# Modulation of the first layer split between TensorE and VectorE, vectors stored as rows, weight splits on ScalarE and GpSimd

## The chip, the cores and the metric

The kernel runs on one core of a Trainium2 chip. The metric is the device time of one execution in microseconds (us). The core's engines are TensorE (PE, with its weight loads PEld), VectorE (DVE), ScalarE (ACT), GpSimd (POOL) and SyncE (SP), which here issues nearly all DMAs. Each engine works through its own queue in order and waits on semaphores of the others.

## The reference

Two layers over 2048 latent tokens and 256 context tokens of width 1024. Cut to what matters here:

```python
silu_c, silu_cc = silu(c), silu(c_ctx)            # two condition vectors, 1024 long
for l in range(2):
    shift, scale, gate = split(silu_c @ w_mod[l] + b_mod[l], 3)        # w_mod[l]: 1024 x 3072
    shift_c, scale_c, gate_c = split(silu_cc @ w_mod[l] + b_mod[l], 3) # the same for the context
    hx = rmsnorm(x, norm_g[l]) * (1 + scale) + shift
    hy = rmsnorm(y, norm_g[l]) * (1 + scale_c) + shift_c
    # hx, hy @ w_in[l]: columns for a Fourier mix, a gated MLP over chunks, and attention (q, k, v, gate)
    # three branches, each times its SiLU gate, concatenated, then
    x = x + gate * (concat(f, g, o) @ w_out[l])
    # and, in the first layer alone, y = y + gate_c * (...)
```

Everything is in float32. The kernel keeps that accuracy by splitting each operand into a high and a low half of fewer bits (`hi` = rounded copy, `lo` = operand minus `hi`) and multiplying three times (high by high, high by low, low by high).

## The kernel before

The kernel is written as a list of operations in program order; a planner (`Plan`) then simulates the engines with a table of costs and writes each engine's queue in the order in which its simulation started the operations. Where several are ready, the one earlier in program order goes first. An operation also needs its tiles: each tile name has a fixed number of buffers in a pool, and a pool opens and closes at a mark that waits until all of its users are done in the plan. So program order is a priority, and a moved statement moves in all queues. Since all instructions are issued by one line of `Plan.emit`, every row of the profile says L447, and groups are told apart by tile names.

A layer runs in stages. *Modulation*: shift (`sh`), scale (`gs`) and gate (`gc`) are made for both conditions `c2` (columns of 128, eight chunks of the 1024, two conditions). *Projection*: tokens go in blocks of 4, 4, 2, 2 and 6 tiles of 128. `norm` loads a tile, normalises it, transposes it on TensorE, applies scale and shift (half on VectorE, half on ScalarE) and splits it; `block` then runs the tile against five groups of weight columns. `group` loads a group of 8 chunks of 128 rows (416, 512, 256, 512 and 512 columns for groups 0 to 4), and `resident` scales each by a power of two (`wr`) taken from the largest entry (`am`, `power`) and splits it in place. Groups 0 and 1 live in tiles called `h`, the others in `w`; the scaled copy is a `k` tile (tiles `k1`, `k2`, `k3` and `k5` all print as `k`). *Attention* follows, with a background of Fourier mixing, the layer's gate vector (`modulate_turned` on VectorE, then `gates`) and, in layer 0, `prepare` for layer 1. *Output*: `outward` projects, multiplies by the gate row `gr` and adds to x; during it `modulate_turned` makes shift and scale for layer 1.

In layer 0 `modulate` makes shift, then scale: for each half of 512 columns eight loads of 128 x 512 weights and eight matmuls with the two conditions as the stationary operand, then a copy and four small transposes back into columns. It is called for shift, then two tiles are fetched ahead, then for scale. `bounded` derives the common scaling. `c_d` and `g_d` are scratch rows in DRAM: conditions and gates are stored there from their column layout, and read back broadcast to all partitions.

In layer 0 program order is then: `norm` of the first four tiles, group 0, and `prepare` (the small weights).

The lines that order the start:

```python
modulate(0, y, (0,), k2)
ahead = {t: fetch(0, t) for t in range(2)}
modulate(0, y, (1,), k2)
...
sp.dma_start(out=c_d[c].rearrange("(k p) -> p k", k=KC), in_=c2[:, :, c])
...
for t in BLOCKS[0][0]:
    hts[t] = norm(0, y, t, ahead.get(t))
wt = {0: group(0, y, 0, wp)}
```

Of the kernel before, what the change touches and what calls it, by code (L numbers as in the profile page):

```python
# [10 lines left out]
F32 = mybir.dt.float32  # L11
F32R = mybir.dt.float32r
F16 = mybir.dt.float16
BF16 = mybir.dt.bfloat16
I32 = mybir.dt.int32
AF = mybir.ActivationFunctionType
ALU = mybir.AluOpType
# [4 lines left out]
P = 128  # L22
# [526 lines left out]
def hybrid_kernel(ctx: ExitStack, tc: tile.TileContext, a: dict, out: bass.AP):  # L549
# [3 lines left out]
    def mk(p, shape, dt, tag, bufs=None):  # L553
        return plan.tile(p, shape, dt, tag, bufs or p.bufs)

    def opened(name, side, bufs=2):
        p = plan.pool(name, bufs=bufs, side=side, reuse_waits="tile")
        p.bufs = bufs
        return p
# [17 lines left out]
    def bank(shape=None, tag="cb"):  # L577
        return mk(stage[0] if tag in ("pj", "cx", "sc") else ps, shape or [P, NB], F32, tag, BANKS[tag])
# [113 lines left out]
    def column(i):  # L692
        return cols[:, i:i + 1]


    NAMES, BASES = ("sh", "gs", "gc"), (C_BSH, C_BSC, C_BG)

    def modulated(l, y, part, ns, sums):

        co = l * C_L  # L700
        dst = y[NAMES[part]]
        b0 = co + BASES[part] + ns.start
        for c in range(2):
            dve.tensor_tensor(out=dst[:, ns, c], in0=sums[:, :, c], in1=cols[:, b0:b0 + ns.stop - ns.start], op=ALU.add)
            if part == 1:
                dve.scalar_tensor_tensor(out=dst[:, ns, c], in0=dst[:, ns, c], scalar=1.0,
                                         in1=cols[:, co + C_G + ns.start:co + C_G + ns.stop], op0=ALU.add, op1=ALU.mult)

    def modulate(l, y, parts, load):

        for part in parts:
            y[NAMES[part]] = mk(lay, [P, KC, 2], F32, NAMES[part], 1)
            for n in range(2):
                row = bank([2, NB])
                for k in range(KC):
                    wm = load()
                    sp.dma_start(out=wm, in_=a["w_mod"][l, k * P:(k + 1) * P, part * D + n * NB:part * D + (n + 1) * NB])
                    pe.matmul(row, c2[:, k, :], wm, start=k == 0, stop=k == KC - 1)
                o = bank([P, 4, 2])
                rs = load()[0:2, :]  # L720
                act.activation(out=rs, in_=row, func=AF.Copy)
                with plan.group():
                    for m in range(4):
                        pe.transpose(o[:, m], rs[:, m * P:(m + 1) * P], ident[0:2, 0:2])
                modulated(l, y, part, slice(4 * n, 4 * n + 4), o)

    def modulate_turned(l, y, parts, load):

        conds = []
        for c in range(2):  # L730
            for n in range(2):
                w = load()
                sp.dma_start(out=w, in_=c_d[c, n * NB:(n + 1) * NB].partition_broadcast(P))
                conds.append(w)
        for part in parts:
            y[NAMES[part]] = mk(lay, [P, KC, 2], F32, NAMES[part], 2 if part == 2 else 1)
            acc = mk(lay, [P, 2, KC, 2], F32, "acc")
            for k in range(KC):
                for n in range(2):
                    wm = load()  # L740
                    sp.dma_start(out=wm, in_=a["w_modT"][l, part * D + k * P:part * D + (k + 1) * P, n * NB:(n + 1) * NB])
                    for c in range(2):
                        jk = k2([P, D], BF16)[:, :NB]
                        dve.scalar_tensor_tensor(out=jk, in0=wm, scalar=1.0, in1=conds[2 * c + n], op0=ALU.mult, op1=ALU.mult,
                                                 accum_out=acc[:, n, k, c:c + 1])
                    yield
            dve.tensor_tensor(out=acc[:, 0], in0=acc[:, 0], in1=acc[:, 1], op=ALU.add)
            modulated(l, y, part, slice(0, KC), acc[:, 0])
# [45 lines left out]
    def whole(v):  # L794

        return v.rearrange("p s n -> p (s n)").bitcast(F32)
# [103 lines left out]
    def fetch(l, t):  # L900
        xt = k5()[:, :D]
        sp.dma_start(out=xt, in_=src(l, t))
        return xt

    def norm(l, y, t, xt=None):
        c = 1 if t < CT else 0
        xt = xt or fetch(l, t)
        jk = k2([P, D], BF16)
        ss = mk(small, [P, 1], F32, "ss")
        act.activation(out=jk, in_=xt, func=AF.Square, accum_out=ss)  # L910
        dve.tensor_scalar(out=ss, in0=ss, scalar1=1.0 / D, scalar2=EPS, op0=ALU.mult, op1=ALU.add)
        rs = rsqrt1(ss)
        dve.tensor_scalar(out=xt, in0=xt, scalar1=rs, scalar2=-1.0, op0=ALU.mult, op1=ALU.mult)
        hh, hl = rows_operand(t)
        for half in range(2):
            tp = bank([P, 4, P], "cx" if half else "cb")
            with plan.group():
                for i in range(4):
                    k = 4 * half + i
                    pe.transpose(tp[:, i], xt[:, k * P:(k + 1) * P], ident)  # L920
            u = k2([P, 4, P])
            for i in range(4):
                k = 4 * half + i
                if half:
                    act.activation(out=u[:, i], in_=tp[:, i], func=AF.Identity, scale=y["gs"][:, k, c:c + 1], bias=y["sh"][:, k, c:c + 1])
                else:
                    dve.tensor_scalar(out=u[:, i], in0=tp[:, i], scalar1=y["gs"][:, k, c:c + 1], scalar2=y["sh"][:, k, c:c + 1],
                                      op0=ALU.mult, op1=ALU.add)
            s = slice(4 * half, 4 * half + 4)
            act.activation(out=hh[:, s], in_=u, func=AF.Copy)  # L930
            pool.tensor_tensor(out=hl[:, s], in0=u, in1=hh[:, s], op=ALU.subtract)
        return hh, hl
# [16 lines left out]
    def resident(y, g, parts, v):  # L949


        am = mk(small, [P, KC + 1], F32, "am", 2)
        for k in range(KC):
            c0 = 0
            for get, c in parts:
                get(k, whole(v(k))[:, c0:c0 + c])
                c0 += c
            dve.tensor_reduce(out=am[:, k:k + 1], in_=whole(v(k)), axis=AX.X, op=ALU.max, apply_absolute_value=True)
        dve.tensor_tensor(out=am[:, :KC], in0=am[:, :KC], in1=y["hi"], op=ALU.mult)
        dve.tensor_reduce(out=am[:, KC:], in_=am[:, :KC], axis=AX.X, op=ALU.max)  # L960
        pw = mk(lay, [P, 2], F32, f"pw{g}")
        power(am[:, KC:], pw)
        y["ic"][g] = pw[:, 1:]
        r = mk(small, [P, KC], F32, "wr", 2)
        dve.tensor_scalar(out=r, in0=y["hi"], scalar1=pw[:, 0:1], scalar2=None, op0=ALU.mult)
        n = v(0).shape[2]
        for k in range(KC):
            w = k2()[:, :n]
            if k % 2:
                dve.tensor_scalar(out=w, in0=whole(v(k)), scalar1=r[:, k:k + 1], scalar2=None, op0=ALU.mult)  # L970
            else:
                act.activation(out=w, in_=whole(v(k)), func=AF.Copy, scale=r[:, k:k + 1])
            act.activation(out=v(k)[:, 0], in_=w, func=AF.Copy)
            (pool if k % 2 else dve).tensor_tensor(out=v(k)[:, 1], in0=w, in1=v(k)[:, 0], op=ALU.subtract)
        return [(v(k)[:, 0], v(k)[:, 1]) for k in range(KC)]

    def weights(parts, wp, scale=None, extra=None):
# [645 lines left out]
    def gates(l, y, pc):  # L1623

        y["gr"] = []
        for c in range(1 if l == DEPTH - 1 else 2):
            sp.dma_start(out=g_d[c].rearrange("(k p) -> p k", k=KC), in_=y["gc"][:, :, c])
            gr = mk(pc, [P, D], F32, f"gr{c}", 1)
            sp.dma_start(out=gr, in_=g_d[c].partition_broadcast(P))
            y["gr"].append(gr)  # L1630
# [10 lines left out]
        sp.dma_start(out=out[(t - CT) * P:(t - CT + 1) * P, ns] if l == DEPTH - 1 else x1_d[t][:, ns], in_=xr)  # L1641


    def run(jobs):
        for _ in jobs:
            pass

    banks("project")
    wp = opened("W", "right")
    pa = opened("A", "left")  # L1650
    y = {}
    modulate(0, y, (0,), k2)
    ahead = {t: fetch(0, t) for t in range(2)}
    modulate(0, y, (1,), k2)
    tt = mk(cst, [P, 2, 256], F32, "tt")
    sp.dma_start(out=tt, in_=a["dft64"])
    for c in range(2):
        sp.dma_start(out=c_d[c].rearrange("(k p) -> p k", k=KC), in_=c2[:, :, c])
    hts = {}
    bounded(y)  # L1660
    pa_[0] = pa
    for t in BLOCKS[0][0]:
        hts[t] = norm(0, y, t, ahead.get(t))
    y["ic"] = [None] * 5
    wt = {0: group(0, y, 0, wp)}
    first = prepare(0, y, wp)
    for _ in range(8):
        next(first)
# [189 lines left out]
```

## Time and profile before

| | |
|---|---|
| runs (3) | median 3200.58 us, 3195.83 to 3202.14 |
| profiled execution | 3200.15 us, span 3198.0 us |
| mean granted TensorE clock | 0.969 |
| busy: TensorE, weight loads | 2978.9 us (93%), 1737.2 us (54%) |
| busy: VectorE, ScalarE, GpSimd | 2463.7 us (77%), 1811.3 us (57%), 1674.5 us (52%) |
| DMA | 291.69 MB, mean 91 GB/s; 377744 of 495312 packets under 512 B |

Busy shares are means over stages with different limits. The first projections begin at about 80 us, layer 0's attention runs from about 640 to 1460 us, layer 1's first projections are at about 1715 us. A view of windows gives busy time by stage; a row of the timeline gives start, duration, engine and operation; the chain that ended last is followed back from the last instruction.

### The profile page before, as it was taken

To read this page: it belongs to the slowest core of one execution; us is meant where nothing else is said; L and a number is where in the kernel's file an instruction comes from. 1 tells how busy PE (TensorE), PEld (TensorE's weight loads), DVE (VectorE), ACT (ScalarE), POOL (GpSimd) and SP (SyncE) were. 2 spreads that over 40 slices of the span, in tenths; PEclk is the share of its full clock that TensorE was granted. 3 is DMA by queue.
4 is the path that set the end of the run, shared out by engine and by line. 5 is a ranking of instruction groups with operands and counts; after the bars stand their busy time and mean duration, and the time that the engine had idled before them with its cause. 6 is when DMAs were issued, how large, how long until landed. Compare 5 with 4: busy or idle time off the path is not lost.

```text
span 3198.0 us, 64363 instructions
## 1 busy us (share of the span) xinstructions
PE 2978.9 (93%) x23200; PEld 1737.2 (54%) x23200; DVE 2463.7 (77%) x6739; ACT 1811.3 (57%) x3860; POOL 1674.5 (52%) x1816
## 2 busy tenths in 40 slices
PE   5799999899999999998999899998999999999899
PEld 1355555445655455556785454553455555555687
DVE  4888788789998978864638988986898989887332
ACT  2553345267677788884005544531787878888500
POOL 1453444457667777772003645542776777777300
PEclk7899999999999999999999999998999999999999
DMA  8323344532224322205535343445123222230342
GB/s 269 61 59 68 71 86 85 104 106 71 73 76 134 71 64 55 77 22 165 180 116 188 57 91 81 88 94 128 36 62 89 72 83 67 75 80 18 111 128 83
DMA packets 495312, 291.69 MB, mean 91 GB/s; under 512 B 377744, under 2 KB 427024, under 8 KB 494992
## 3 DMA queue, kind: packets, MB, share of 16 engines
q1 hardware_dynamic: 492112, 282.34, 34.3%
q0 software_dynamic: 2880, 5.24, 0.6%
q8 instruction: 182, 2.98, 0.4%
q14 instruction: 138, 1.13, 0.1%
HBM read 195.80 MB, written 91.66 MB: 90 GB/s over the span
## 4 chain that ended last, share of the span: by engine, by line
PE 58%; DVE 20%; DMA 9%; ACT 6%; POOL 3%; SPq 3%; issue 2%; DVEq 0%; ACTq 0%; POOLq 0%
PE pj L447 17%; PE sc L447 17%; PE pv L447 11%; PE mx L447 9%; DVE k L447 6%; DVE mx L447 3%; PE cb L447 3%; SPq L447 3%; DMA k<-d 2%; ACT k L447 2%; DVE ns_t L447 1%; POOL k L447 1%; ACT pp L447 1%; DMA k<-in_x_dram 1%; DMA mw<-in_w_modT_dram 1%
## 5 line engine op out<-in xcount | busy, mean ns | idle before, releaser
L447 POOL TENSOR_TENSOR pp<-pw,pp 128x512 f16<-128x512 f32 (+1 forms) x876 | 1021.3, 1183 | 390.0 <-ACT pw L447 313.6
L447 PEld LDWEIGHTS <-h 128*128 128x128 f16 (+2 forms) x7008 | 577.5, 97 | 778.9 <-issue 412.4
L447 DVE TENSOR_REDUCE mx<-mx 128x1 f32<-128x512 f32 (+1 forms) x1296 | 772.6, 626 | 151.2 <-PE mx L447 144.7
L447 ACT ACTIVATE pp<-sc 128x512 f16<-128x512 f32 (+1 forms) x1168 | 716.5, 614 | 243.2 <-PE sc L447 218.0
L447 PE MATMUL sc<-h,h 128*128 128x512 f16 (+1 forms) x2336 | 602.3, 380 | 3.9 <-ACT pw L447 2.1
L447 ACT ACTIVATE pw<-sc 128x512 f32<-128x512 f32 (+1 forms) x876 | 542.7, 620 | 0.6 <-POOL pp L447 0.6
L447 PEld LDWEIGHTS <-pp 128*128 128x128 f16 x10432 | 468.5, 98 | 115.5 <-issue 27.8
L447 PE MATMUL pv<-k,pp 128*128 128x65 f16 (+2 forms) x10432 | 508.3, 203 | 9.2 <-DVE sm L447 7.6
L447 PE MATMUL mx<-h,h 96*128 96x512 f16 (+1 forms) x1296 | 409.5, 367 | 40.0 <-DVE mx L447 25.3
L447 PE MATMUL pj<-wh,h 128*128 128x512 f32 x1088 | 362.9, 406 | 7.9 <-DVE k L447 7.8
L447 PEld LDWEIGHTS <-hp 128*128 128x128 f16 x1920 | 189.6, 100 | 179.0 <-issue 24.6
L447 PE MATMUL pj<-w,h 128*128 128x512 f16 (+1 forms) x1296 | 271.5, 348 | 5.4 <-DVE tm L447 2.1
L447 PE MATMUL pj<-w,hp 128*128 128x512 f16 (+1 forms) x1152 | 244.4, 348 | 10.7 <-DVE tm L447 3.8
L447 PEld LDWEIGHTS pj<-wh,h 128*128 128x128 f32 x1088 | 208.5, 192 | 58.1 <-DVE k L447 11.8
L447 DVE TENSOR_TENSOR pp<-sc,pp 128x512 f16<-128x512 f32 (+1 forms) x292 | 197.9, 678 | 45.1 <-ACT sc L447 41.2
L447 PE MATMUL sc<-h 40*128 40x512 f16 (+1 forms) x1168 | 227.7, 387 | 0.0
L447 PE MATMUL pj<-wl,h 128*128 128x512 f32 x544 | 216.7, 398 | 0.0
L447 PE MATMUL pj<-h,h 128*128 128x416 f16 (+2 forms) x912 | 197.7, 357 | 9.4 <-DVE h L447 5.2
L447 ACT ACTIVATE k<-pj,pw 128x256 f32<-128x256 f32 (+3 forms) x242 | 105.2, 458 | 178.4 <-PE pj L447 166.6
L447 POOL TENSOR_TENSOR h<-k,h 128x512 f16<-128x512 f32 (+1 forms) x56 | 66.4, 1199 | 263.1 <-ACT h L447 263.0
L447 DVE TENSOR_TENSOR pj<-pj,gr 128x512 f32<-128x512 f32 x68 | 47.3, 697 | 190.3 <-PE pj L447 190.3
L447 PE MATMUL pj<-h,hp 128*128 128x416 f16 (+1 forms) x768 | 176.3, 369 | 8.8 <-ACT k L447 5.4
(260 smaller groups left out, 4013.5 us busy)
## 6 DMA issues: line engine op xcount, KB each, us to landing
d<-k SPq DMA_DIRECT2D x560, 48.0 KB
d<-k SPq DMA_DIRECT2D x166, 128.0 KB
d<-k SPq DMA_DIRECT2D x70, 256.0 KB
k<-d SPq DMA_DIRECT2D x132, 128.0 KB
k<-d SPq DMA_DIRECT2D x66, 256.0 KB
h<-d SPq DMA_DIRECT2D x24, 432.0 KB
d<-vt SPq DMA_DIRECT2D x144, 65.0 KB
k<-d SPq DMA_DIRECT2D x16, 585.0 KB
```

The lines of the kernel that those rows point to most:

```text
L447: r = getattr(getattr(self.nc, eng), method)(*args, **kw)
```

## The change

The first layer's shift is no longer a row of matmuls: both conditions are spread to all partitions (identity scaled by each chunk, times a matrix of ones, into four PSUM banks), and VectorE multiplies rows of the transposed weights (`w_modT`) with them and sums along the row. Scale stays on TensorE. One load brings 128 x 1024 weights instead of 128 x 512, from a pool of its own (`pm`, ten buffers) that closes ahead of the pool `wp` for weights. The broadcast conditions also give the rows for `c_d`, and gates are transposed on TensorE so that `g_d` is written in pieces of 128 numbers. `resident` scales all chunks on ScalarE and subtracts all on GpSimd. Group 0 stands ahead of the norms in program order, and no tile is fetched ahead.

```diff
-    def modulate(l, y, parts, load):
-        for part in parts:
+    def modulate(y, load):
+        conds = [bank(tag=tag) for tag in ("mx", "mx", "pj", "pj")]
+        for i in range(2 * KC):
+            dg = k1()[:, :P]
+            dve.tensor_scalar(out=dg, in0=ident, scalar1=c2[:, i % KC, i // KC:i // KC + 1], scalar2=None, op0=ALU.mult)
+            pe.matmul(conds[i // 4][:, i % 4 * P:(i % 4 + 1) * P], ones, dg, start=True, stop=True)
+        for i, o in enumerate(conds):
+            r = k2()[0:1]
+            act.activation(out=r, in_=o[0:1], func=AF.Copy)
+            sp.dma_start(out=c_d[i // 2, i % 2 * NB:(i % 2 + 1) * NB].unsqueeze(0), in_=r)
...
+        halves = [bank([2, NB], "cx" if n else "pv") for n in range(2)]
+        for k in range(KC):
+            wm = load()
+            sp.dma_start(out=wm, in_=a["w_mod"][0, k * P:(k + 1) * P, D:2 * D])
             for n in range(2):
...
+                pe.matmul(halves[n], c2[:, k, :], wm[:, n * NB:(n + 1) * NB], start=k == 0, stop=k == KC - 1)
+            wm = load()
+            sp.dma_start(out=wm, in_=a["w_modT"][0, k * P:(k + 1) * P])
+            for i in range(4):
+                c, n = i // 2, i % 2
+                dve.scalar_tensor_tensor(out=k2([P, D], BF16)[:, :NB], in0=wm[:, n * NB:(n + 1) * NB], scalar=1.0, in1=conds[i],
+                                         op0=ALU.mult, op1=ALU.mult, accum_out=acc[:, n, k, c:c + 1])
+        dve.tensor_tensor(out=acc[:, 0], in0=acc[:, 0], in1=acc[:, 1], op=ALU.add)
+        modulated(0, y, 0, slice(0, KC), acc[:, 0])
...
+    def scattered(v, d, n):
+        tp = bank([KC * 2, P])
+        pe.transpose(tp, v.rearrange("p k c -> p (k c)"), ident)
+        r = k1()[:KC * 2, :P]
+        act.activation(out=r, in_=tp, func=AF.Copy)
+        for c in range(n):
+            sp.dma_start(out=d[c].rearrange("(k p) -> k p", k=KC), in_=r[c::2])
...
     def modulate_turned(l, y, parts, load):
...
+        cs = [load() for _ in range(4)]
+        for i, w in enumerate(cs):
+            sp.dma_start(out=w, in_=c_d[i // 2, i % 2 * NB:(i % 2 + 1) * NB].partition_broadcast(P))
...
# resident
-            if k % 2:
-                dve.tensor_scalar(out=w, in0=whole(v(k)), scalar1=r[:, k:k + 1], scalar2=None, op0=ALU.mult)
-            else:
-                act.activation(out=w, in_=whole(v(k)), func=AF.Copy, scale=r[:, k:k + 1])
+            act.activation(out=w, in_=whole(v(k)), func=AF.Copy, scale=r[:, k:k + 1])
             act.activation(out=v(k)[:, 0], in_=w, func=AF.Copy)
-            (pool if k % 2 else dve).tensor_tensor(out=v(k)[:, 1], in0=w, in1=v(k)[:, 0], op=ALU.subtract)
+            pool.tensor_tensor(out=v(k)[:, 1], in0=w, in1=v(k)[:, 0], op=ALU.subtract)
...
# gates
-            sp.dma_start(out=g_d[c].rearrange("(k p) -> p k", k=KC), in_=y["gc"][:, :, c])
+        scattered(y["gc"], g_d, n)
...
# start of the program
-    wp = opened("W", "right")
...
-    modulate(0, y, (0,), k2)
-    ahead = {t: fetch(0, t) for t in range(2)}
-    modulate(0, y, (1,), k2)
+    pm = opened("M", "right")
+    modulate(y, lambda: mk(pm, [P, D], F32, "wm", 10))
+    plan.close(pm)
+    wp = opened("W", "right")
...
-    for c in range(2):
-        sp.dma_start(out=c_d[c].rearrange("(k p) -> p k", k=KC), in_=c2[:, :, c])
...
-    for t in BLOCKS[0][0]:
-        hts[t] = norm(0, y, t, ahead.get(t))
...
     wt = {0: group(0, y, 0, wp)}
+    for t in BLOCKS[0][0]:
+        hts[t] = norm(0, y, t)
```

More of the change, by code (lines that the diff above doesn't have):

```diff
@@ L693, in column, with run @@
         return cols[:, i:i + 1]
+    def run(jobs):
+        for _ in jobs:
+            pass
     NAMES, BASES = ("sh", "gs", "gc"), (C_BSH, C_BSC, C_BG)
@@ L707, in modulated @@
                                          in1=cols[:, co + C_G + ns.start:co + C_G + ns.stop], op0=ALU.add, op1=ALU.mult)
-    def modulate(l, y, parts, load):
-        for part in parts:
-            y[NAMES[part]] = mk(lay, [P, KC, 2], F32, NAMES[part], 1)
-            for n in range(2):
[L714 to L725, printed above, removed]
@@ L727, in modulate_turned @@
-    def modulate_turned(l, y, parts, load):
-        conds = []
-        for c in range(2):
[L731 to L734, printed above, removed]
+    def modulate(y, load):
[8 more added lines that the diff above has]
+            sp.dma_start(out=c_d[i // 2, i % 2 * NB:(i % 2 + 1) * NB].unsqueeze(0), in_=r)
+        for part in range(2):
+            y[NAMES[part]] = mk(lay, [P, KC, 2], F32, NAMES[part], 1)
+        acc = mk(lay, [P, 2, KC, 2], F32, "acc")
+        halves = [bank([2, NB], "cx" if n else "pv") for n in range(2)]
+        for k in range(KC):
+            wm = load()
+            sp.dma_start(out=wm, in_=a["w_mod"][0, k * P:(k + 1) * P, D:2 * D])
+            for n in range(2):
+                pe.matmul(halves[n], c2[:, k, :], wm[:, n * NB:(n + 1) * NB], start=k == 0, stop=k == KC - 1)
[7 more added lines that the diff above has]
+        modulated(0, y, 0, slice(0, KC), acc[:, 0])
+        for n in range(2):
+            o = bank([P, 4, 2])
+            rs = k2()[0:2, :]
+            act.activation(out=rs, in_=halves[n], func=AF.Copy)
+            with plan.group():
+                for m in range(4):
+                    pe.transpose(o[:, m], rs[:, m * P:(m + 1) * P], ident[0:2, 0:2])
+            modulated(0, y, 1, slice(4 * n, 4 * n + 4), o)
@@ L743, in modulate_turned @@
                         jk = k2([P, D], BF16)[:, :NB]
-                        dve.scalar_tensor_tensor(out=jk, in0=wm, scalar=1.0, in1=conds[2 * c + n], op0=ALU.mult, op1=ALU.mult,
+                        dve.scalar_tensor_tensor(out=jk, in0=wm, scalar=1.0, in1=cs[2 * c + n], op0=ALU.mult, op1=ALU.mult,
                                                  accum_out=acc[:, n, k, c:c + 1])
@@ L1625, in gates @@
         y["gr"] = []
-        for c in range(1 if l == DEPTH - 1 else 2):
-            sp.dma_start(out=g_d[c].rearrange("(k p) -> p k", k=KC), in_=y["gc"][:, :, c])
+        n = 1 if l == DEPTH - 1 else 2
+        scattered(y["gc"], g_d, n)
+        for c in range(n):
             gr = mk(pc, [P, D], F32, f"gr{c}", 1)
@@ L1641, in outward @@
         sp.dma_start(out=out[(t - CT) * P:(t - CT + 1) * P, ns] if l == DEPTH - 1 else x1_d[t][:, ns], in_=xr)
-    def run(jobs):
-        for _ in jobs:
-            pass
     banks("project")
-    wp = opened("W", "right")
     pa = opened("A", "left")
     y = {}
-    modulate(0, y, (0,), k2)
-    ahead = {t: fetch(0, t) for t in range(2)}
-    modulate(0, y, (1,), k2)
+    pm = opened("M", "right")
+    modulate(y, lambda: mk(pm, [P, D], F32, "wm", 10))
+    plan.close(pm)
+    wp = opened("W", "right")
     tt = mk(cst, [P, 2, 256], F32, "tt")
     sp.dma_start(out=tt, in_=a["dft64"])
-    for c in range(2):
-        sp.dma_start(out=c_d[c].rearrange("(k p) -> p k", k=KC), in_=c2[:, :, c])
     hts = {}
```

## The prediction

> **What bounds the kernel now.** I read the chain that ended last first, restricted to the start of the span (columns: start us, us, what).
>
> ```profile
> 2.06 2.78 DMA k<-in_w_mod_dram
> 4.98 5.26 PE cb L447 x9
> 10.24 14.15 DMA k<-in_w_mod_dram
> ...
> 57.67 4.06 DMA k<-in_x_dram
> 61.80 5.87 DMA k<-in_x_dram
> ```
>
> The start waits for DMA: once for modulation weights, for 14.15 us, and later for two x tiles. The timeline says what was in the queue and when the stages ended.
>
> ```profile
> 7.67 2.47 SPq L447 DMA_DIRECT2D d<-c  x2
> ...
> 54.15 0.16 DVE L447 TENSOR_TENSOR gs<-cb,cols 128x4 f32<-128x4 f32 x1 [1.94 <-PE cb L447]
> ...
> 56.38 0.16 DVE L447 TENSOR_TENSOR sh<-sh,hb 128x8 f32<-128x8 f32 x1
> ...
> 79.67 0.50 PE L447 MATMUL pj<-h,h 128*128 128x416 f16 x1 [1.79 <-ACT h L447]
> 80.13 4.79 POOL L447 TENSOR_TENSOR h<-k,h 128x416 f16<-128x416 f32 x4 [2.31 <-ACT h L447]
> ```
>
> `d<-c` is the store of the conditions, element by element. Bandwidth from 8 to 26 us, in 40 slices of 0.45 us:
>
> ```profile
> GB/s 337 351 382 414 391 373 346 410 410 387 334 95 34 6 1 0 0 0 5 18 9 105 14 18 18 23 27 9 9 36 41 91 96 86 332 350 344 382 403 383
> ```
>
> 23 slices, 13.0 to 23.3 us, are nearly empty, and around them loads run at about 375 GB/s. So some 10 us of the 14.15 are that store, and shift and scale are final only at 56.5 us; the first projection starts 23 us after that. Then the engines by stage:
>
> ```profile
> core 0: us, PE busy (x) PEld busy (x) DVE busy (x) ACT busy (x) POOL busy (x), PEclk, DMA share, GB/s
> 0.00:56.50 56.50, 35.98 (x88) 7.81 (x88) 20.37 (x82) 6.65 (x12) 1.58 (x12) 0.87 0.84 263
> 56.50:104.00 47.50, 30.91 (x157) 19.17 (x158) 31.51 (x137) 33.26 (x77) 22.35 (x29) 0.72 0.48 162
> 104.00:140.00 36.00, 15.32 (x57) 8.21 (x56) 35.91 (x124) 18.19 (x40) 18.77 (x27) 0.73 0.38 71
> 140.00:230.00 90.00, 86.40 (x471) 46.35 (x471) 78.66 (x261) 46.32 (x99) 47.28 (x53) 0.98 0.30 59
> 1714.00:1832.00 118.00, 100.64 (x518) 52.49 (x516) 108.39 (x381) 68.49 (x153) 62.40 (x83) 0.91 0.37 94
> ```
>
> From 104 to 140 VectorE is full (35.91 of 36) and TensorE waits for it; from 140 on TensorE is the bound (86.40 of 90). Layer 1 has a like stretch at 1714 to 1832: VectorE 108.39 of 118, TensorE idle for 17.4.
>
> **The change, part by part.**
>
> Modulation of layer 0. The bytes stay: 8.39 MB, 22.4 us at 375 GB/s, now in 16 loads in place of 32. The gap of 10 us goes. Half of the 32 row matmuls go from TensorE. VectorE gets 32 sums over 512; the same instruction of layer 1, with operands in SBUF, is the nearest row (64 in this stretch), and a VectorE instruction of that shape that reads PSUM stands below it, then the parts of the conditions' broadcast (scaling ident, then ones times it).
>
> ```profile
> 1476.00:1568.00 92.00, 41.05 (x128) 0.93 0.72 225
> ```
>
> ```profile
> L447 DVE SCALAR_TENSOR_TENSOR vt<-mx,vt 128x512 f16<-128x512 f32 x8 | 5.4, 679 | 0.0
> ...
> L447 PE MATMUL cb<-wf,ones 128*128 128x128 f32 x8 | 1.6, 287 | 0.3 <-DVE n_y L447 0.3
> ...
> L447 DVE TENSOR_SCALAR wf<-ident,vs 128x128 f32<-128x128 f32 x4 | 1.2, 300 | 3.9 <-POOL uq L447 3.7 <-POOL uk L447 0.2
> ```
>
> 41.05/64 = 0.64 us each, so 32 take 20.5 us (bounds 19 to 22 from 0.60 to 0.68; I take 0.64, the same instruction). The broadcast is 16 steps of 0.30 on VectorE and two matmul records of 0.287 each, with three buffers: 16 x 0.4 = 6.5 us, from about 3 us, when the conditions are there, to 10. Sums without a gap then end at 30.5; the last load lands at 2 + 2.8 + 22.4 = 27, so VectorE, not DMA, sets the end. In between it also does the eight maxima of group 0 (0.614 each, row below: 4.9 us). From the last sum to the final shift takes what it takes now from 54.15 to 56.54, 2.4 us. That gives 38 us in place of 56.5: 18.5 us earlier. Bounds: 33 (maxima elsewhere) and 46 (sums at 0.85 through waits for loads).
>
> From there to the end of the VectorE stretch. Before, 56.5 to 140 holds 31.51 + 35.91 = 67.4 us of VectorE work and 16.1 idle. Off it come the operands of groups 0 and 1:
>
> ```profile
> L447 DVE TENSOR_REDUCE am<-h x16: 580/614/678, 26.3 to 119.7; 128x1 f32<-128x416 f32 x8, 128x1 f32<-128x512 f32 x8
> L447 DVE TENSOR_SCALAR k<-h,wr x8: 415/442/474, 78.1 to 144.5; 128x416 f32<-128x416 f32 x4, 128x512 f32<-128x512 f32 x4
> L447 DVE TENSOR_TENSOR h<-k,h x8: 568/658/2087, 79.9 to 143.9; 128x416 f16<-128x416 f32 x4, 128x512 f16<-128x512 f32 x4
> ```
>
> 8 x 0.442 + 8 x 0.658 = 8.8 us. Onto it comes what VectorE did ahead of 56.5 in its idle time and now does later: of 20.4 us, some 5 are modulation and its tail, 5 the maxima, the rest, about 10 (norms of the two early tiles, `prepare`), is put off. Work: 67.4 - 8.8 + 10 = 69 us. Idle: the power step of group 0 comes ahead of the norms, so the two x waits (9.9 us) no longer stand before the first projection, but GpSimd now feeds group 0 alone, 8 x 1.2 = 9.6 us where four took 4.79; the two early x tiles load after group 0's weights and the other two still wait for buffers. I take 12 of idle (16 as now, 8 if all fits). End: 38 + 69 + 12 = 119 for 140: **-21 us** (bounds -12 and -30).
>
> Groups 2 to 4 of layer 0:
>
> ```profile
> L447 ACT ACTIVATE k<-w,wr x12: 492/708/722, 145.5 to 200.3; 128x512 f32<-128x512 f32 x8, 128x256 f32<-128x256 f32 x4
> L447 DVE TENSOR_SCALAR k<-w,wr x12: 339/478/1459, 145.7 to 216.3; 128x512 f32<-128x512 f32 x8, 128x256 f32<-128x256 f32 x4
> L447 POOL TENSOR_TENSOR w<-k,w x12: 672/1155/1679, 147.1 to 217.8; 128x512 f16<-128x512 f32 x8, 128x256 f16<-128x256 f32 x4
> L447 DVE TENSOR_TENSOR w<-k,w x12: 410/676/1235, 147.8 to 214.5; 128x512 f16<-128x512 f32 x8, 128x256 f16<-128x256 f32 x4
> ```
>
> VectorE loses 12 x (0.478 + 0.676) = 13.8 us, ScalarE gains 12 x 0.708 = 8.5 on 46.3 of 90, GpSimd 12 x 1.155 = 13.9 on 47.3. TensorE has 3.6 us to win, and loses where a group comes later: four more subtractions in GpSimd's line, 4 x 1.155 = 4.6 us a group. I take **-1** (bounds -3.6 and +12).
>
> Layer 1 does the same 40 moved instructions: VectorE loses about 22.6 us in the stretch where TensorE idles 17.4. No modulation changes there. I take a third of the idle, less than one late group: **-5** (bounds -12 and +14, three groups 4.6 late).
>
> Gates. Now the element store of two rows holds SyncE's queue until it has landed:
>
> ```profile
> 1068.94 2.20 SPq L447 DMA_DIRECT2D d<-gc x2
> ...
> 1078.42 2.38 SPq L447 DMA_DIRECT2D gr<-d x2
> ```
>
> ```profile
> 1080.00:1090.00 10.00, 7.14 (x58) 4.29 (x59) 8.75 (x26) 4.32 (x10) 3.81 (x4) 0.83 0.85 217
> ```
>
> The next head's loads queue behind it and TensorE loses 2.9 us; the rows go out at once now. Against that a transpose in TensorE's order waits for the gate sums, with score matmuls behind it, 0.3 us and a wait, twice, and a ScalarE copy of 16 rows. I take **0** net (bounds -3 and +2). `modulate_turned` allocates its four condition tiles first: 0, the same loads in the same order.
>
> Sum: -21 - 1 - 5 + 0 = -27 on the profiled execution's 3200.15, which lies 0.4 under the median of 3200.58: **3173 us**.
>
> **A rule against the change.** How far TensorE waits for GpSimd's operand rows now, from 80 to 260 us and then from 1714 to 1832 (view of the waits: us in total, times, longest):
>
> ```profile
> PE pj L447 <- POOL w L447: 1.0, 1, 1.0
> ```
>
> ```profile
> PE pj L447 <- POOL w L447: 2.2, 3, 1.2
> ```
>
> The rows above show VectorE's subtraction stretched from a median of 0.676 to 1.235 and from 0.658 to 2.087 us while GpSimd works. The Trainium skill, "SBUF — State Buffer", section "SBUF: two separate sides", says that VectorE and GpSimd share a port pair as an exclusive lock, held for a whole instruction, against VectorE instructions with two SBUF inputs among others. By that rule the trace agrees, and moving work to GpSimd takes time back from VectorE's other instructions, which is the first rival's sum, 3189. By the medians, and since the subtractions that stretched are themselves the ones removed, it stays 3173.
>
> **Rivals.**
>
> *VectorE is held up by GpSimd's new work.* Each of the 40 added GpSimd instructions stretches one VectorE instruction by 1.235 - 0.676 = 0.56 us; the 28 that fall in VectorE-bound stretches (8 and 20) cost 28 x 0.56 = 16 us: 3173 + 16 = 3189. For: the two maxima. Against: the medians lie near the minima.
>
> *The sums fill VectorE until late.* Loads come interleaved with group 0's weights, sums at 0.85 us, shift final at 46 and idle 16 as now: 46 + 69 + 16 = 131, -9 in place of -21, in all -15: 3185. For: 26 us of new work on the engine that is full at 104. Against: before that VectorE idles for 52 us of 104.
>
> *GpSimd sets the pace (slower).* Ten groups, each 3 to 5 us later: per layer 8 x 1.2 + 12 x 1.155 = 23.5 us, 47 in all, on the path if nothing covers them: -21 + 47 = +26, 3226. It decides against the change once more than 21 of the 47, say five groups of ten, are waited for. For: a tile's projection takes eight weight chunks one after the other, and GpSimd makes one per 1.2 us. Against: the waits just quoted, 1.0 and 2.2 us, and GpSimd's 47.3 of 90.
>
> *It doesn't do what it says:* another order of the plan's instructions returns the gain later, within 6 us of 3200.
>
> **How the numbers follow.** A measurement here can tell about 0.2%, 6.4 us. Chances: forecast 0.52 (3173), held up 0.12 (3189), late sums 0.19 (3185), unchanged 0.08, GpSimd's pace 0.09. Faster: 0.52 + 0.12 + 0.19 = 0.83; same 0.08; slower 0.09. The forecast's own range, with the groups' bounds taken half, is 3155 to 3186; the rivals that are faster lie inside 3196. So 3154 to 3196, which leaves out the last two cases and a few hundredths below.
>
> **What would show it.** Right: no empty slices of bandwidth before 30 us; `sh<-sh,hb` last at 36 to 40 us; the first `pj` near 45; VectorE's full stretch ends near 119; no `DVE ... <-k,w` rows; TensorE's idle time at layer 1's start under 15 us. Wrong: shift final after 46 us; `PE pj <- POOL h` or `POOL w` waits of over 10 us in a layer; first projections that still wait for x tiles; a gain present at 140 us and gone by 640.

## The result, and the profile after

| | before | after |
|---|---|---|
| runs (4 each, one chip) | median 3199.81 us, 3195.83 to 3202.14 | median 3163.47 us, 3161.06 to 3165.14 |
| ratio | | 0.9887, 95% interval 0.987 to 0.9904 |
| profiled execution | 3200.15 us, span 3198.0 us | 3161.06 us, span 3159.3 us |

The change takes 36 us off, 1.1%, and it lies in the predicted range. The profiled execution of after is the fastest of its four, so the spans differ by 38.7 us, a little more than the medians. The head of its page:

```profile
span 3159.3 us, 64415 instructions
PE 2967.6 (94%) x23194; PEld 1737.5 (55%) x23194; DVE 2447.3 (77%) x6738; ACT 1833.8 (58%) x3904; POOL 1707.2 (54%) x1856
```

The engine totals hardly move: VectorE -16 us, ScalarE +23, GpSimd +33, and TensorE's 2978.9 is now 2967.6. What moves is when work can start. The bandwidth from 0 to 40 us, in slices of 1 us:

```profile
GB/s 0 31 81 150 360 422 397 426 406 426 422 397 418 406 418 205 324 401 356 393 414 401 422 410 408 381 381 376 376 380 415 406 363 219 340 302 354 358 336 261
```

From 4 us on no slice falls under 205 GB/s; the hole at 13 to 23 us is gone. The timeline then has the last of the sums over the transposed weights, the last step of the shift, and the first long row of projections:

```profile
31.00 0.68 DVE L447 SCALAR_TENSOR_TENSOR k<-wm,pj 128x512 bf16<-128x512 f32 x1
...
38.00 0.16 DVE L447 TENSOR_TENSOR sh<-sh,hb 128x8 f32<-128x8 f32 x1
...
52.20 7.97 PE L447 MATMUL pj<-h,h 128*128 128x416 f16 x33
```

The shift is final at 38.2 us where it was at 56.5. Engines by stage (start:end, length, then busy us and count of PE, PEld, DVE, ACT, POOL, granted clock, DMA share, GB/s):

```profile
0.00:38.30 38.30, 21.97 (x72) 8.45 (x72) 30.32 (x117) 7.41 (x13) 0.44 (x8) 0.88 0.93 346
38.30:104.00 65.70, 46.95 (x202) 27.81 (x203) 51.23 (x218) 43.10 (x103) 33.12 (x47) 0.76 0.52 162
104.00:120.00 16.00, 5.98 (x18) 1.94 (x17) 15.49 (x52) 6.86 (x12) 8.02 (x11) 0.71 0.25 38
120.00:140.00 20.00, 19.87 (x88) 9.10 (x88) 17.27 (x57) 14.18 (x34) 14.80 (x20) 0.89 0.40 69
140.00:230.00 90.00, 81.31 (x453) 44.36 (x451) 66.49 (x226) 50.13 (x103) 56.49 (x65) 0.96 0.31 66
1690.00:1808.00 118.00, 108.69 (x558) 56.48 (x559) 100.24 (x361) 81.39 (x179) 84.37 (x110) 0.94 0.37 93
```

VectorE's full stretch (15.49 of 16) now ends at 120, and TensorE is full from there (19.87 of 20). But from 140 to 230 TensorE is busy for 81.31 of 90 where it was 86.40: part of the lead is lost again. When the second block of tokens starts, at 231.2 us for 245.2, 14.0 us of the 20.3 are left, and by the first scores there are 20.5 again. In layer 1's stretch TensorE's idle time goes from 17.4 to 9.3 us. The chain that ended last, after first and then before, has the same two marks:

```profile
46.32 4.79 DMA w<-in_w_g_dram
...
54.87 6.26 DMA k<-in_x_dram
...
120.13 13.11 PE pj L447 x50
```

```profile
140.38 12.91 PE pj L447 x50
```

The long run of projections starts 20.3 us earlier, and one x load still stands on the way.

To say where the rest went, I take four stages from the timelines: from the start to layer 0's first scores (`sc`), from there to layer 1's first projection, from that to layer 1's first scores, and the rest. In the profile of before they are 661.0, 1055.2, 529.5 and 952.3 us long. The table has the difference of each kernel's profiled span to them; executions of one kernel lie up to 13 us apart (e1, 3161.24 to 3174.51), so the medians decide and a single profile only says in which stage to look. Times of a stage further down are from such single profiles.

| us against before | to scores, layer 0 | to layer 1 | layer 1 to scores | rest | span | median, ratio [95%] |
|---|---|---|---|---|---|---|
| after | -20.5 | -3.6 | -14.3 | -0.3 | -38.7 | 3163.47, 0.9887 [0.987, 0.9904] |
| e1 change, old splits | -26.4 | -0.6 | +0.9 | -4.3 | -30.4 | 3166.55, 0.9901 [0.9885, 0.9917] |
| e2 new splits alone | +0.9 | +3.9 | -12.8 | -1.2 | -9.2 | 3188.66, 0.9967 [0.9957, 0.9978] |
| e3 rows alone | -6.3 | -3.2 | -2.8 | -0.9 | -13.2 | 3190.8, 0.9978 [0.9969, 0.9986] |
| e4 shift on TensorE | -20.5 | -2.2 | -17.2 | -4.4 | -44.3 | 3163.38, 0.9886 [0.9872, 0.9901] |
| e5 norms first | -12.5 | +0.9 | -19.4 | -2.0 | -33.0 | 3166.64, 0.9898 [0.9882, 0.9915] |
| e6 gates by element | -18.5 | -1.5 | -15.6 | -0.7 | -36.3 | 3165.83, 0.99 [0.9885, 0.9914] |
| e7 group 4 shared | -15.8 | +0.5 | -14.4 | +0.9 | -28.8 | 3169.8, 0.9904 [0.9889, 0.9919] |
| e8 new splits in layer 1 only | -30.3 | -0.1 | -11.5 | +3.3 | -38.6 | 3156.01, 0.9865 [0.985, 0.9881] |
| e9 change, third x buffer | -31.5 | -3.9 | -21.2 | -2.0 | -58.6 | 3144.05, 0.9829 [0.9815, 0.9842] |
| e10 e8, third x buffer | -36.5 | +2.7 | -19.2 | -1.8 | -54.8 | 3144.15, 0.9827 [0.9813, 0.984] |
| e11 e4 and e10 together | -27.8 | +2.3 | -21.9 | -3.8 | -51.2 | 3148.37, 0.9843 [0.983, 0.9857] |
| e12 before, third x buffer | -25.8 | +3.9 | -9.8 | +2.2 | -29.5 | 3169.18, 0.9907 [0.9893, 0.9922] |

### The profile page after: what moved, and what is told of

The parts are those of the page before. It is cut to its first block, busy times and chain, and to the rows that moved or that the text cites. A ratio compares the mean times of both kernels' runs of the same rounds, so it can differ in the third digit from the quotient of the medians.

```text
span 3159.3 us, 64415 instructions
## 1 busy us (share of the span) xinstructions
PE 2967.6 (94%) x23194; PEld 1737.5 (55%) x23194; DVE 2447.3 (77%) x6738; ACT 1833.8 (58%) x3904; POOL 1707.2 (54%) x1856
## 4 chain that ended last, share of the span: by engine, by line
PE 61%; DVE 18%; DMA 8%; ACT 6%; POOL 3%; issue 2%; SPq 2%; DVEq 0%; ACTq 0%; POOLq 0%
PE pj L447 21%; PE sc L447 17%; PE pv L447 11%; PE mx L447 9%; DVE k L447 5%; DVE mx L447 3%; DMA k<-d 3%; PE cb L447 2%; ACT k L447 2%; SPq L447 2%; ACT pp L447 2%; DMA k<-in_x_dram 1%; DMA mw<-in_w_modT_dram 1%; POOL k L447 1%; ACT pw L447 1%
## 5 line engine op out<-in xcount | busy, mean ns | idle before, releaser
L447 PE MATMUL pj<-w,hp 128*128 128x512 f16 (+1 forms) x1152 | 238.8, 349 | 10.9 <-DVE tm L447 7.2
L447 POOL TENSOR_TENSOR h<-k,h 128x512 f16<-128x512 f32 (+1 forms) x72 | 81.4, 1146 | 297.2 <-ACT h L447 296.1
```

The source lines that it names most:

```text
L447: r = getattr(getattr(self.nc, eng), method)(*args, **kw)
```

## The experiments

### Which part carries the gain (e1 to e4)

**e1: the change with the old splits.** ScalarE and VectorE scale in turn, VectorE and GpSimd subtract in turn, as before.

```diff
# after.py, resident
-            act.activation(out=w, in_=whole(v(k)), func=AF.Copy, scale=r[:, k:k + 1])
+            if k % 2:
+                dve.tensor_scalar(out=w, in0=whole(v(k)), scalar1=r[:, k:k + 1], scalar2=None, op0=ALU.mult)
+            else:
+                act.activation(out=w, in_=whole(v(k)), func=AF.Copy, scale=r[:, k:k + 1])
             act.activation(out=v(k)[:, 0], in_=w, func=AF.Copy)
-            pool.tensor_tensor(out=v(k)[:, 1], in0=w, in1=v(k)[:, 0], op=ALU.subtract)
+            (pool if k % 2 else dve).tensor_tensor(out=v(k)[:, 1], in0=w, in1=v(k)[:, 0], op=ALU.subtract)
```

> The changed kernel with the weight splits shared with VectorE as before (scaling and subtraction of every second chunk). Theory A (VectorE's relief through the splits is worth about 14 us in layer 1's projections and some 6 us of the start): 3178 to 3186 us, shift final still at 38 us, layer 1's VectorE stretch as long as before. Rival B (the late gain comes from another order of the plan, not from VectorE's relief): 3163 to 3170 us, layer 1's projections as short as in the changed kernel.

Measured 3166.55, 3 us over the change, with intervals that overlap. So nearly all of the 36 us is there without the new splits, and the reading that put the kernel at 3178 to 3186 fell in its total. In the stages it held for layer 1 (+0.9 in place of -14.3) and was wrong for layer 0, where the old splits reach the scores 6 us earlier (-26.4).

**e2: before with the new splits alone** (the same edit the other way, in the kernel before).

> The kernel before with the new splits alone (all scaling on ScalarE, all subtraction on GpSimd). Theory A: 3177 to 3186 us, the gain in layer 1's projections (about 14 us) and in layer 0's VectorE stretch at 104 to 140 us. Rival B: within 6 us of the kernel before. Rival of the prediction (GpSimd sets the pace): 3205 us or more, with TensorE waiting for GpSimd's operand rows.

Measured 3188.66, -10.7 us against its own median of before (3199.35). That lies in none of the three ranges. All of it stands in layer 1 (-12.8), as theory A had it; in layer 0 the long run of projections starts 8.5 us earlier (131.9 for 140.4), but nothing of it is left at the scores, which theory A had wrong. The first stretch of layer 1, from the first projection to the end of group 3's first block, in before, e1 and e2, one fence each:

```profile
1716.20:1812.10 95.90, 82.91 (x435) 44.70 (x435) 86.30 (x300) 55.80 (x130) 50.87 (x69) 0.90 0.39 100
```

```profile
1689.20:1785.90 96.70, 83.71 (x436) 45.03 (x436) 86.37 (x300) 55.89 (x131) 50.92 (x69) 0.90 0.39 100
```

```profile
1721.00:1799.70 78.70, 75.88 (x417) 41.17 (x417) 69.29 (x253) 56.73 (x133) 56.13 (x79) 0.97 0.41 108
```

Before and e1 agree within 1 us; with the new splits VectorE has 17 us less to do there and the stretch is 17 us shorter. TensorE's idle time in it falls from 13.0 to 2.8 us. The other 7 us are its busy time: 18 matmul records fewer lie ahead of this mark, and its granted clock is 0.97 where it was 0.90.

**e3: before with the conditions stored as rows.**

```diff
# before.py
-    for c in range(2):
-        sp.dma_start(out=c_d[c].rearrange("(k p) -> p k", k=KC), in_=c2[:, :, c])
+    scattered(c2, c_d, 2)
```

> The kernel before, with the conditions alone stored as rows (one transpose on TensorE, one copy, two stores of eight pieces). Theory A: the empty 10 us of DMA go, shift and scale are final at about 46 us in place of 56.5, and 6 to 10 us of it reach the end: 3190 to 3194 us. Rival C (that store is the whole gain of the start): 3176 to 3182 us. A third (the x waits and VectorE's stretch cover it): 3197 us or more.

Measured 3190.8 (-8.5). The bandwidth from 8 to 26 us, in the slices of 0.45 us that the prediction showed for before:

```profile
GB/s 355 300 319 355 332 364 428 382 396 422 362 380 401 416 392 396 396 394 370 376 386 378 382 405 382 381 390 392 375 388 377 377 386 370 382 392 410 379 385 343
```

No slice is empty, and the shift is final at 45.6 us, 10.9 earlier. The store by element was the hole, and it alone is worth 8.5 us of the run (interval 4.5 to 9.9).

**e4: the change with the shift on TensorE**, from the same pool, in the same stream of loads; conditions stored as rows; no sums on VectorE.

```diff
# after.py, modulate
-            wm = load()
-            sp.dma_start(out=wm, in_=a["w_modT"][0, k * P:(k + 1) * P])
-            for i in range(4):
...
-                dve.scalar_tensor_tensor(...)
+            for part in range(2):
+                wm = load()
+                sp.dma_start(out=wm, in_=a["w_mod"][0, k * P:(k + 1) * P, part * D:(part + 1) * D])
+                for n in range(2):
+                    pe.matmul(halves[2 * part + n], c2[:, k, :], wm[:, n * NB:(n + 1) * NB], start=k == 0, stop=k == KC - 1)
```

> The changed kernel with the shift made by TensorE as well, from the same pool of large loads, and the conditions stored as rows by a transpose. Theory A (the gain of the start is the store's gap, the large loads in one pass and the order, not the sum on VectorE): shift and scale final at 33 to 38 us, VectorE has 26 us less to do there, 3152 to 3166 us. Rival D (the sum on VectorE is what brings it): 3172 us or more, TensorE's 64 row matmuls setting the end of modulation after 40 us.

Measured 3163.38, the change's own time. Its start, to where the shift is final:

```profile
0.00:43.00 43.00, 32.27 (x85) 7.62 (x86) 9.96 (x54) 6.29 (x12) 0.45 (x8) 0.97 0.94 344
```

The total is theory A's. The shift is not: it comes 4.6 us later than in the change (42.8), outside of theory A's 33 to 38 and after the 40 us that the rival had named. VectorE has 20 us less work there, the long run of projections starts at 118.7 us (120.1 in the change), and at the scores of layer 0 the two stand level (-20.5 each). So summing on VectorE brings nothing of itself. What is left for the start is the pool of its own, the larger loads in one pass, the order and the rows; of these the rows have a run of their own (e3) and the order has e5, but the pool and the larger loads were not run alone.

### The order of the start and the gates (e5, e6)

**e5: the norms ahead of group 0 in program order.**

```diff
# after.py
-    y["ic"] = [None] * 5
-    wt = {0: group(0, y, 0, wp)}
     for t in BLOCKS[0][0]:
         hts[t] = norm(0, y, t)
+    y["ic"] = [None] * 5
+    wt = {0: group(0, y, 0, wp)}
```

> The changed kernel with the norms of the first four tiles ahead of group 0 in program order, as before. Theory A (VectorE's stretch up to 140 us sets the end of the start, not the first projection): the first projection comes 5 us or more later, the gain at the first scores shrinks by 0 to 5 us: 3161 to 3169 us. Rival: the order is what brings the start: 3172 us or more.

Measured 3166.64, 3 us over the change, within the intervals. The first projection starts at 68.8 us in place of 52.2, and the first scores come 8 us later, more than the 0 to 5 expected; the way to layer 1 costs 4.5 more and layer 1 gives 5 back. Starting 16.6 us earlier is worth at most 8. The long run of projections starts at the same time in both (120.6 and 120.1 us), and what VectorE does between the shift and that run is nearly the same, 67.8 and 66.8 us of work.

**e6: the gates stored by element, as before.**

```diff
# after.py, gates
-        scattered(y["gc"], g_d, n)
         for c in range(n):
+            sp.dma_start(out=g_d[c].rearrange("(k p) -> p k", k=KC), in_=y["gc"][:, :, c])
```

> The changed kernel with the gates stored element by element as before. Theory A: the store holds the queue for 9 us in attention, but the profile after shows no more than 3 us of it there: 3162 to 3167 us. Rival: the rows are worth more (head loads behind the store): 3169 us or more.

Measured 3165.83, within the intervals of the change; the stage that holds the gates is 2.1 us longer in its profile. Too small to tell from nothing. That the queue no longer stops is seen in the view of its waits. Before, from 1060 to 1084 us, it has (total, times, longest)

```profile
SPq L447 <- DMA d<-gc: 8.2, 2, 6.6
```

In the change, from 1040 to 1060 us, it has no wait for a store, and the reads behind the stores issue as

```profile
1053.56 0.89 SPq L447 DMA_DIRECT2D gr<-d  x2
...
1057.51 0.79 SPq L447 DMA_DIRECT2D h<-d  x2
```

### Where layer 0 gives its lead back (e7, e8)

**e7: group 4 alone keeps the shared splits**, in both layers. **e8: the new splits in layer 1 only.** Both are the edit of e1 under a condition.

```diff
# after.py, resident
+            if not (COND) and k % 2:
+                dve.tensor_scalar(...)
+            else:
                 act.activation(...)
...
+            (pool if (COND) or k % 2 else dve).tensor_tensor(...)   # e7: COND is g < 4; e8: COND is l (layer 1)
```

> The changed kernel, with group 4's splits (the last group, 512 columns) shared with VectorE as before, groups 0 to 3 as changed. Theory G (the gain of the splits is given back because GpSimd's line for group 4, eight subtractions and other work, comes last in both layers): layer 1's lead of some 16 us ahead of group 4 stays, layer 0 keeps 4 to 8 us more at the first scores: 3145 to 3156 us. Rival H (the lead is lost in the next block for another reason, norms or stores): 3159 to 3168 us.

> The changed kernel with the new splits in layer 1 alone, layer 0 shared as before. From the profiles so far: 26 us ahead at the first scores as without any new split, and 14 us in layer 1's projections as in the changed kernel: 3154 to 3161 us. Rival B (layer 1's gain hangs on the order that the plan happens to find, not on the splits): 3163 to 3170 us.

e7 measured 3169.8, above both ranges and 6 us over the change, with intervals that overlap: no gain, so a late group 4 in GpSimd's line is not seen to be where the lead goes. e8 measured 3156.01, 7 us under the change, with intervals that overlap a little; its layer 0 is 10 us ahead of the change's (-30.3) and its layer 1 keeps -11.5. So the new splits are worth 12 to 15 us in layer 1 and, beside the rest of the change, cost 6 to 10 in layer 0 (1 in e2, without it). The ratios of the medians say 11.5 for layer 1 (e8 against e1) and 7 for layer 0 (the change against e8). Why they cost there is not settled: e4 has them in layer 0 as well and goes from the end of group 3's first block to the second in 34.8 us, where the change takes 41.9 and e8 35.9. Each kernel has another order of plan, and no run separates that from the splits.

### What still waits: the x tiles (e9 to e12)

x tiles (`k<-in_x_dram`) go through a tile name with two buffers. **e9** is the change with three:

```diff
# after.py, the x tiles
-        return mk(main, [P, NT * 65], F32, "k5")
+        return mk(main, [P, NT * 65], F32, "k5", 3)
```

**e10** is e8 with it, **e11** e4 with it and with the new splits in layer 1 only, **e12** the kernel before with it and nothing else.

> The changed kernel with three buffers in place of two for the tiles that x is loaded into (k5). Theory X (the lead that the splits give in layer 1 is lost in the next block because an x tile's load starts late and ScalarE's queue waits for it, 6.8 us on the chain at 1820 us, as at 55 us in the start): 8 us of the 40 at group 3 are no longer given back, 3148 to 3157 us. Rival Y (ScalarE and GpSimd are full and give the lead back whatever the loads do): 3160 to 3168 us.

> The new splits in layer 1 alone, with three x buffers. Theory X: 3143 to 3152 us. Rival Y: 3152 to 3161 us, as with two buffers.

> The same as the one before, with the shift made by TensorE from the large loads. If the sum on VectorE brings nothing, as the run with that alone suggests: within 5 us of the one before. If VectorE's 26 us matter where the splits of layer 0 are on VectorE again: 5 us or more faster.

> The kernel before with three x buffers alone. If the third buffer works on what the change uncovered (x loads that came late only once the stretches ahead were shorter): 3189 to 3198 us, most of it from the x waits at 57 to 68 us. If it is a gain of its own, whatever the change does: 3178 to 3186 us, as much as the 19 us that it brought to the changed kernel.

e9 measured 3144.05 and e10 3144.15, 19 us under the change and 55 us under before: the fastest kernels of the study, e9 4 us below the range of theory X. e11 (3148.37) is no better. With three buffers e8's advantage over the change is gone. And the third buffer is no matter of this change alone: in the kernel before it takes off 31 us (e12, 3169.18 against 3200.4 on its chip), more than either expectation. 36 and 31 would make 67; together they make 55, so the two have some 12 us in common.

The first two loads of x tiles in the change, then in e9 (rows of SP's queue):

```profile
44.05 0.33 SPq L447 DMA_DIRECT2D k<-in_x_dram  x1
...
54.87 0.36 SPq L447 DMA_DIRECT2D k<-in_x_dram  x1
```

```profile
28.87 0.33 SPq L447 DMA_DIRECT2D k<-in_x_dram  x1
...
43.95 0.33 SPq L447 DMA_DIRECT2D k<-in_x_dram  x1
```

ScalarE's wait for such loads to the end of layer 0's projections (0 to 640 us; total, times, longest), again the change and e9:

```profile
ACT k L447 <- DMA k<-in_x_dram: 21.7, 7, 5.6
```

```profile
ACT k L447 <- DMA k<-in_x_dram: 15.1, 6, 5.5
```

In e9 the loads are issued 11 to 15 us earlier and the wait falls by 6.6 us; the first projection starts no earlier (52.0 us), and 9 of the 11 us by which layer 0 then leads the change come after the second block. In e12 it hardly falls (26.2 to 25.5), yet layer 0 gains 25.8, some 20 of it after the second block. From there to the first scores, before and e12:

```profile
245.20:661.00 415.80, 388.07 (x2119) 207.50 (x2117) 337.62 (x1240) 154.97 (x369) 178.33 (x266) 0.98 0.42 87
```

```profile
239.00:635.20 396.20, 380.70 (x2119) 205.39 (x2116) 325.48 (x1213) 155.41 (x364) 179.36 (x263) 0.99 0.42 92
```

The matmuls are the same 2119; TensorE's idle time falls from 27.7 to 15.5 us and its busy time by 7. VectorE does 27 instructions fewer in this stage: a reading that fits is that with a further buffer the plan starts work on a tile earlier and TensorE finds its operands ready more often. How much of this is the buffer and how much the order that the planner then finds, these runs don't say.

## Why the prediction was right, and which terms were off

**Start: -21, measured -20.3.** The hole of 10 us goes (e3). The sums over the transposed weights start 0.61 us apart, where I took 0.64: 28 of them begin between 14.58 and 31.00 us without a gap, each 0.68 us long in its row, so a row overlaps the next. The shift is final at 38.2 us (predicted 38). VectorE's stretch ends at 120.1 (119), with 66.8 us of work since the shift (69) and 15.0 idle (12).

Off is the first projection, 52.2 for "near 45". It is of a context tile, and no x load stands before it, as forecast: the x load of 6.26 us on the chain is issued at 54.87. What TensorE waits for ahead of it is ScalarE:

```profile
51.29 1.12 PE L447 MATMUL cx<-ident,k 128*128 128x128 f32 x4 [3.51 <-ACT k L447]
```

From 41.45 to 49.8 us ScalarE makes the scalings and roundings of group 0, and only then reads the tile's transposed columns. The forecast had reckoned GpSimd's pace there and left out ScalarE's. e5 shows that this miss costs little.

One step of the sum did not hold, although the total did: that the splits take 8.8 us off VectorE's stretch. e1 leaves them on VectorE, has its shift final at 38.5 us, and still starts the long run of projections at 116.6, 3.5 us ahead of the change, with 68.8 us of VectorE work and 9.6 idle. So beside the rest of the change the splits took off 2 us of work and added 5 of idle time; that the sum met 119 is in part luck. And the credit is to be read rightly: e4 reaches the same time without VectorE's sums, so what I costed as a price (26 us of new work on VectorE) was paid from its idle time and bought nothing that the time shows.

**Groups 2 to 4 of layer 0: -1, measured -0.2** at the scores. That is luck: at the second block, where these groups are over, 6.3 us of the lead are gone, inside the bound of +12 but far from the -1, and the 6.5 us that return by the scores come in blocks for which I had forecast nothing. Without the splits the kernel stands 11.6 us better at the second block (e1, 219.6 us) and 6 to 10 at the scores (e1, e8).

**Layer 1: -5, measured -14.3.** This is the term that was mis-sized, by 9 us, a little outside its lower bound. I took a third of TensorE's idle time, for fear of late groups. The change's stretch, beside the rows of before, e1 and e2 above:

```profile
1692.10:1772.60 80.50, 76.58 (x416) 41.34 (x416) 70.42 (x252) 56.67 (x132) 56.03 (x79) 0.96 0.40 103
...
1786.00:1806.00 20.00, 16.16 (x64) 6.57 (x62) 13.22 (x42) 17.64 (x34) 19.06 (x19) 0.83 0.19 56
```

The first 80.5 us reach the mark that took 95.9: 9.1 of TensorE's 13.0 us of idle time are won, not a third of them. The other 6.3 are busy time, and 19 matmul records fewer lie ahead of the mark, so part of that is work put off. Then comes what I feared: for 20 us GpSimd is full (19.06) and stands on the chain, and TensorE idles for 3.8 of them:

```profile
1790.56 5.68 POOL w L447 x5
```

Further on, at 1829.7 us, is a wait of TensorE for ScalarE that before does not have (total, times, longest):

```profile
PE pv L447 <- ACT vv L447: 4.5, 1, 4.5
```

At the second block, with nearly as many matmul records behind it in both (680 and 675), the lead of this stage is 4.5 us (141.2 for 145.7), 4.3 of it idle time: close to the -5. So the forecast held up to there, and the step that failed is the one after it: the other 10 us of the 14.3 come between the second block and the first scores, a stretch that the term put at nothing. Five of them are idle time at the turn to attention. TensorE's wait there for the first head's loads, in before, the change and e1 (total, times, longest):

```profile
PE mx L447 <- DMA h<-d: 6.4, 1, 6.4
```

```profile
PE mx L447 <- DMA h<-d: 1.5, 1, 1.5
```

```profile
PE mx L447 <- DMA h<-d: 6.2, 1, 6.2
```

The other five are busy time: from the second block to the scores TensorE is busy for 351.58 us before and 347.00 in the change, with 1901 and 1907 records, at a granted clock of 0.95 and 0.97. The last head loads stand in SP's queue after other stores of projections than before. With the new splits alone (e2) the wait is 1.2, and e12, without any new split, has it at 2.6. So it can go without the new splits; whether they or the order that the plan finds with them shorten it in the change stays open, since no run changes this order alone.

**Gates: 0, measured within noise** (e6). **Rest: 0, measured -3.6 and -0.3.**

So the forecast of 3173 came out 10 high: -20.3 - 0.2 - 3.6 - 14.3 - 0.3 = -38.7 in place of -27, and 9 of the 12 are layer 1's term.

**The rivals.** *GpSimd's pace* (3226) needed five late groups of ten. TensorE's waits for GpSimd's operands in the change, from 80 to 260 us and then from 1690 to 1840:

```profile
PE pj L447 <- POOL w L447: 1.2, 1, 1.2
...
PE pj L447 <- POOL h L447: 0.7, 1, 0.7
```

```profile
PE pj L447 <- POOL w L447: 1.9, 2, 1.3
```

These waits are as small as before. The ones that grew in layer 0 are for ScalarE, which no rival named: `PE pj <- ACT h` goes from 1.8 to 5.0 us and `PE pj <- ACT w` from 0.6 to 2.4. The e4 kernel has the same splits and waits 2.3 for both together, so this too depends on the order. *VectorE held up* (3189) did not come: e2, with the splits alone, is faster. *Late sums* (3185) did not come either: 38.2 and not 46. *Unchanged* did not come for the whole; the splits taken by themselves are close to it (3 us between e1 and the change).

## What to carry to other kernels

Look for holes in the stream of loads at the start first: a small store by element held the queue for 10 us, and writing it as rows was worth about as much as moving 40 operations of each layer between engines (8.5 and 10.7 us, e3 and e2). When VectorE bounds a stretch, work moved off it may pay there (17 us less work, 10 us less idle time of TensorE in e2's layer 1) or not (layer 0's start, e1 against the change), and what stays at the end is what the next stage does not give back; compare the lead at several marks, with the same work behind each. And before engines are rebalanced, try the buffer count of the tile whose loads stand in the chain: one more buffer was worth 31 us of the kernel before, nearly as much as the whole change.

## What the runs showed of the hardware that was not expected

The prediction showed GpSimd's subtraction in layer 0 with a median of 1.155 and a maximum of 1.679 us, and took VectorE to be the one held up. In the kernel before, the longest one starts 0.01 us behind one of VectorE's own subtractions:

```profile
192.31 0.68 DVE L447 TENSOR_TENSOR w<-k,w 128x512 f16<-128x512 f32 x1
192.32 1.68 POOL L447 TENSOR_TENSOR w<-k,w 128x512 f16<-128x512 f32 x1
```

In the change the tile's row from 0 to 330 us is

```profile
L447 POOL TENSOR_TENSOR w<-k,w x24: 667/1155/1165, 136.1 to 197.8; 128x512 f16<-128x512 f32 x16, 128x256 f16<-128x256 f32 x8
```

Twice as many, the same median, and the maximum is down to 1.165, with VectorE's own subtractions out of `resident`. In the other kernels with the new splits in layer 0 the maximum there is 1.16 to 1.34 (e2, e4, e9), with the old ones 1.48 to 1.68 (e1, e8, e12), so most of the stretch goes with those subtractions. GpSimd is held up too, which agrees with the exclusive lock of the Trainium skill, "SBUF — State Buffer", section "SBUF: two separate sides", where whichever instruction starts first holds the ports. The rival drawn from that rule counted the stretch of VectorE's instructions and left out, unlike the forecast, that the change takes out those that contend.
